# Gates and matrix-memory scores as three one-pass products, and the sample's key and query rows written before the gates

## The chip, the cores and the metric

The kernel runs on one core of one Trainium2 chip. The metric is the device time of one execution in microseconds (us). The time before is the median of three runs, 1539.87 us (1538.17 to 1540.1). Engines are called as the profile calls them: PE (matrix products), PEld (its weight loads), DVE (vector), ACT (scalar and activation functions), POOL, and SP, which here only issues DMAs.

## What is computed

One layer of a hybrid decoder, for a prompt of 256 tokens and a batch of 8 sample tokens: 264 columns together, in single precision. The parts that the change touches are the recurrent group (RG-LRU) and the mLSTM group, which share one projection `z = xn @ w_in`:

```python
xr, conv_new = causal_conv(z[..., OFF_RGX:OFF_RGG], conv_buf, conv_w, conv_b)
r = jax.nn.sigmoid(block_diag(xr, w_rg_a, b_rg_a))
ig = jax.nn.sigmoid(block_diag(xr, w_rg_x, b_rg_x))
h_rg, h_last = rglru(xr, r, ig, rg_lambda, h0)
y_rg = rmsnorm(h_rg * jax.nn.gelu(z[..., OFF_RGG:OFF_Q]), g_rg_out)
...
qk = jnp.einsum('bhtd,bhsd->bhts', qc, kc) * D
num = sc[..., None] * jnp.einsum('bhtd,bhdv->bhtv', qc, C) + jnp.einsum('bhts,bhsv->bhtv', qk, vc)
C_new = dec[..., None, None] * C + jnp.einsum('bhs,bhsd,bhsv->bhdv', w_end, kc, vc)
...
y_ml = rmsnorm(h_ml, g_ml_out) * jax.nn.sigmoid(z[..., OFF_O:OFF_I])
x = x + jnp.concatenate([y_rg, y_ml], axis=-1) @ w_out
```

`block_diag` is 8 blocks of 128 x 128 for each of the two gates. After this come cross attention to a memory of 256 tokens, a SwiGLU feed-forward part and a last norm.

## The kernel before

Everything is held transposed: 128 features on the partitions, the 264 tokens along the row. All large products run over weights that stream from HBM, in a list `steps` of 128-column blocks of 2048 rows. SP loads a step as two **pieces** of 1024 columns (tile `raw`, 5 buffers). ACT copies a piece to fp32r (the high part) and DVE subtracts to get the low part; both land in one tile `W`, of which there are **4 buffers**. PE then makes three one-pass fp32r products for each 128 x 128 block (`mm3`: high x high, high x low, low x high), 24 for a piece. A product of two plain fp32 tiles is also possible; the profile records it as two matmuls. I count pieces from 0: step s uses pieces 2s and 2s + 1, and because the ring has four tiles, piece n + 4 can be written only after PE has read all of piece n.

`w_in` is steps 0 to 40: 0 to 7 the RG-LRU input, 8 the mLSTM gates, 9 to 16 queries and keys, 17 to 24 values, 25 to 32 the gelu branch, 33 to 40 the mLSTM output gate. Results leave PSUM through DVE (`evac_...`).

Everything else runs as side threads (`side`, generators), which the step loop pumps: `pump` lets a thread go on while DVE's and ACT's estimated clocks are less than `SLACK` ahead of PE's. So the amount of side work decides in which step a thread's next part is issued. A scheduler then fixes one order of instructions for each engine, and each engine works through its order. Work with high priority (the splits above all) is moved forward. The threads that matter:

- `rg_gen` (L524): convolution `rg_conv`, the gates (16 fp32 products, two for each of 8 blocks), sigmoids, exponentials, square roots, scans.
- `ml_gates`, `ml_prompt` (the prompt's scores, two fp32 products for each head), `ml_values`, `ml_heads`.
- `ml_sample` (L815): the 8 sample tokens. It forms kd = key x input gate, transposes kd and the query to rows, writes them to HBM (`scr`) and reads them back spread over all partitions (`fetch`), and updates the matrix memory C for each head.
- `ml_norm` (L880), started at step 24 with the highest priority. It waits until `ml_heads` and `ml_sample` are done and step 33 is reached. Then it hands PE three kinds of small products by a queue of "drips", each due after so many further chunks of a step: `sums` (four, one for each head), `turn` (one, 19 chunks later: it transposes the normalising factor `f` to rows), and `scale` (four, 6 chunks later and then one each: they spread the rows `hl` that ACT and DVE make of `turn`'s result).

Two lines bind these drips to the steps. In `proj`, a step's first chunk is issued after the last drip:

```python
if c == 0:
    d = st.get("edge")
```

And `evac_o(j)` cannot go on without the scaled heads. It drains the queue if need be:

```python
finish(lambda: ml.get("nn", 0) > j // 2)
```

The loop holds the results of steps 33 to 35 back and evacuates them together after step 36's products (`if i == 36`). Whatever is left of the drips is then issued at once, in front of step 37.

Of the kernel before, what the change touches and what calls it, by code (L numbers as in the profile page):

```python
# [10 lines left out]
F32 = mybir.dt.float32  # L11
# [10 lines left out]
NS = 8  # L22
# [68 lines left out]
def layer_kernel(ctx: ExitStack, tc, xT, memT, vec, wrg, w_in, w_out, w_q, w_k, w_v, w_o,  # L91
# [398 lines left out]
    def evac_rgx(n):  # L490
        def f(ps):
            if "xr" not in rg:
                rg["xr"] = Arr(RGB)
            z = B([P, 2, 292])
            zi = z[:, 0, :]
            dve.memset(zi[:, 0:3], 0.0)
            smp = zi[:, 259:291].rearrange("p (b j) -> p b j", j=4)
            hist = V("cst", n * 24, 24).rearrange("p (b j) -> p b j", j=3)
            act.activation(smp[:, :, 0:3], hist, AF.Copy)
            dve.tensor_mul(zi[:, 3:259], ps[:, :T], rstd[:, :T])  # L500
            dve.tensor_mul(smp[:, :, 3:4], ps[:, T:N].rearrange("p (b j) -> p b j", j=1),
                           rstd[:, T:N].rearrange("p (b j) -> p b j", j=1))
            rg["z", n] = z
            if n >= 4:
                rg["zn"] = n + 1
        return f

    def rg_conv(n):
        z = rg.pop(("z", n))
        zi, t = z[:, 0, :], z[:, 1, :]  # L510
        smp = zi[:, 259:291].rearrange("p (b j) -> p b j", j=4)
        act.activation(cpo[:, n, :], zi[:, 256:259], AF.Copy)
        act.activation(cso[:, n, :, :], smp[:, :, 1:4], AF.Copy)
        w = [V("cw", j * 8 + n) for j in range(4)]
        dve.tensor_scalar(t[:, :288], zi[:, 0:288], w[0], V("cb", n), op0=OP.mult, op1=OP.add)
        dve.scalar_tensor_tensor(t[:, :288], zi[:, 1:289], w[1], t[:, :288], op0=OP.mult, op1=OP.add)
        dve.scalar_tensor_tensor(t[:, :288], zi[:, 2:290], w[2], t[:, :288], op0=OP.mult, op1=OP.add)
        xr = rg["xr"](n)
        dve.scalar_tensor_tensor(xr[:, :T], zi[:, 3:259], w[3], t[:, :T], op0=OP.mult, op1=OP.add)
        ts = t[:, 259:291].rearrange("p (b j) -> p b j", j=4)  # L520
        dve.scalar_tensor_tensor(xr[:, T:N].rearrange("p (b j) -> p b j", j=1), smp[:, :, 3:4], w[3],
                                 ts[:, :, 0:1], op0=OP.mult, op1=OP.add)

    def rg_gen():  # L524
        wr = [B([P, 8, P]), B([P, 8, P])]
        for j in range(2):
            sp.dma_start(wr[j], wrg[:, j * 8: j * 8 + 8, :])
        r, ig = Arr(RGB), Arr(RGB)
        for n in range(RGB):
            while rg["zn"] <= n:  # L530
                yield STEP
            rg_conv(n)
            yield STEP
            for t, j, b in ((r, 0, "ba"), (ig, 1, "bx")):
                ps = bank("ax")
                pe.matmul(ps[:, :N], wr[j][:, n, :], rg["xr"](n), start=True, stop=True)
                last = act.activation(t(n), ps[:, :N], AF.Sigmoid, bias=V(b, n))
            yield 0.1
        yield STEP
        xr, c = rg["xr"], rg["c"]  # L540
        e2 = Arr(RGB)

        for q in range(2):
            for n in range(4 * q, 4 * q + 4):
                with tc.issue_after(last.ins):
                    act.activation(e2(n), r(n), AF.Exp, scale=c[:, 8 + n: 9 + n])
                    le = act.activation(r(n), r(n), AF.Exp, scale=c[:, n: n + 1])
            dve.tensor_scalar(e2.tile(q), e2.tile(q), 1.0, -1.0, op0=OP.min, op1=OP.add)
            dve.tensor_mul(ig.tile(q), ig.tile(q), xr.tile(q))
            yield 2.0  # L550
        rg["le"] = le
        while "emc" not in ml:
            yield STEP
        for q in range(2):
            with tc.issue_after(ml["emc"].ins):
                act.activation(e2.tile(q), e2.tile(q), AF.Sqrt, scale=-1.0)
            dve.tensor_mul(ig.tile(q), ig.tile(q), e2.tile(q))
            yield 1.2
        h = Arr(RGB)
        rg["h"] = h  # L560
        for n in range(RGB):
            dve.tensor_tensor_scan(h(n)[:, :T], r(n)[:, :T], ig(n)[:, :T], 0.0, op0=OP.mult, op1=OP.add)
            yield 0.6
        h0 = V("h0", 0, 64).rearrange("p (n b) -> p n b", b=NS)
        for q in range(2):
            hq, rq_, iq = (t.tile(q)[:, :, T:N] for t in (h, r, ig))
            dve.tensor_mul(hq, rq_, h0[:, 4 * q: 4 * q + 4, :])
            dve.tensor_add(hq, hq, iq)
            act.activation(hlast[:, 4 * q: 4 * q + 4, :], h.tile(q)[:, :, T - 1: N], AF.Copy)
        pool_e.dma_start(o_h, hlast)  # L570
        pool_e.dma_start(o_cp, cpo)
        pool_e.dma_start(o_cs, cso)
        yield 0.3
# [106 lines left out]
    def evac_qk(j):  # L680
        def f(ps):
            if j == 0:
                ml["qk"] = Arr(8)
            if j < 4:
                dve.tensor_mul(ml["qk"](j), ps[:, :N], rstd)
            else:
                dve.scalar_tensor_tensor(ml["qk"](j), ps[:, :N], KSCALE, rstd, op0=OP.mult, op1=OP.mult)
            if j == 7:
                ml["sg"] = side(ml_sample(), 3)
                side(ml_prompt(), 2)  # L690
                side(ml_values(), 2)
                ml["pg"] = side(ml_heads(), 2)
        return f
# [8 lines left out]

    hT = {}

    def ml_prompt():
        qk = ml["qk"]
        yield STEP
        kt = B([P, 2, H, P])
        for tb in range(2):
            ps = bank("ax")  # L710
            for h in range(H):
                pe.transpose(ps[:, h * P: h * P + P], qk(4 + h)[:, tb * P: tb * P + P], ident)
            act.activation(kt[:, tb].rearrange("p h d -> p (h d)"), ps, AF.Copy)
            yield STEP
        while "gates" not in ml or not ml["gates"].done:
            yield STEP
        mhl = ml["mhl"]
        for h in range(H):
# [2 lines left out]
            pe.matmul(bc[:, :T], sel, mhl[:, 0], start=True, stop=False)  # L721
            pe.matmul(bc[:, :T], sel, mhl[:, 1], start=False, stop=True)
            sps = bank("ax")
            q, k = qk(h), qk(4 + h)
            pe.matmul(sps[:, 0:256], k[:, 0:P], q[:, 0:T], start=True, stop=True)
            pe.matmul(sps[:, 256:384], k[:, P:T], q[:, P:T], start=True, stop=True)
            w = B([P, 1024])
            E, Pm, kw = w[:, 0:384], w[:, 384:768], w[:, 768:1024]
            ml["w", h] = (Pm, kw, E[:, 0:P])
# [81 lines left out]

    snew = const.tile([P, H, NS], F32, name="snew")
    nums = const.tile([P, 8, NS], F32, name="nums")

    def ml_sample():  # L815
        while not ml["gates"].done:
# [1 line left out]
        qk = ml["qk"]  # L818
        ks, qs = qk.tile(1)[:, :, T:N], qk.tile(0)[:, :, T:N]
        sc, Dg = bcs[:, :, 0:8], bcs[:, :, 8:16]  # L820
        x = ltmp(64)
        kd, qc = (x[:, o: o + 32].rearrange("p (h b) -> p h b", b=NS) for o in (0, 32))
        dve.tensor_mul(kd, ks, Dg)
        dve.tensor_copy(qc, qs)
        n0 = V("n0", 0, 32).rearrange("p (h b) -> p h b", b=NS)
        dve.tensor_mul(snew, n0, sc)
        dve.tensor_add(snew, snew, kd)
        pool_e.dma_start(o_sn, snew)

        qn_ = ltmp(152)  # L830
        dve.memset(qn_[:, 0:120], 0.0)
        dve.tensor_mul(qn_[:, 120:152].rearrange("p (h b) -> p h b", b=NS), snew, qc)
        yield 0.6
        yield STEP
        ps = bank("ax")
        for h in range(H):
            pe.matmul(ps[:, h: h + 1], qn_[:, 8 * h: 8 * h + P], ones[:, 0:1], start=True, stop=True)
        pe.transpose(ps[0:64, 128:256], x, ident)
        yield STEP
        rows = ltmp(128)  # L840
        act.activation(rows[0:64, :], ps[0:64, 128:256], AF.Copy)
        act.activation(den.rearrange("p (h j) -> p h j", j=3)[:, :, 2:3],
                       ps[:, 0:4].rearrange("p (h j) -> p h j", j=1), AF.Abs)
        scr = drm.tile([64, P], F32, name="scr")
        pool_e.dma_start(scr, rows[0:64, :])
        yield 0.5
        def fetch(h, b4):
            C, kq = B([P, 4, 2, P]), B([P, 2, 4, P])
            pool_e.dma_start(C, c0T[h, :, b4 * 4: b4 * 4 + 4])
# [3 lines left out]
                pool_e.dma_start(kq[:, j].rearrange("p b d -> p (b d)"), src.partition_broadcast(P))  # L853
            return C, kq

        ahead = fetch(0, 0)
        yield STEP
        for h in range(H):
            while ml.get("vn", 0) < 2 * h + 2:
                yield STEP  # L860
            for b4 in range(2):
                C, kq = ahead
                n = 2 * h + b4 + 1
# [2 lines left out]
                for bb in range(4):  # L866
                    b = b4 * 4 + bb
                    t2 = tmp(256).rearrange("p (v d) -> p v d", d=P)
                    for vb in range(2):
                        act.activation(t2[:, vb, :], kq[:, 0, bb, :], AF.Copy,  # L870
                                       scale=ml["v"](2 * h + vb)[:, T + b: T + b + 1])
                    dve.scalar_tensor_tensor(C[:, bb], C[:, bb], sc[:, h, b: b + 1], t2, op0=OP.mult, op1=OP.add)
                    for vb in range(2):
                        dve.scalar_tensor_tensor(t2[:, 0, :], C[:, bb, vb, :], 1.0, kq[:, 1, bb, :], op0=OP.mult,
# [744 lines left out]
```

## Time and profile before

| | |
|---|---|
| time, median of 3 runs | 1539.87 us (1538.17 to 1540.1) |
| the profiled execution's own time | 1535.74 us |
| its span in the trace | 1534.0 us |
| busy: DVE, ACT, POOL | 69%, 51%, 8% of the span |
| DMA, mean | 215 GB/s |

The span is what the trace covers from the first to the last instruction; the profiled execution's own time is 1.74 us longer. An entry "A <- B: us, times, longest" in the waits says that A's engine sat idle until B finished. In the chain of waits and in the timeline a row is a start, a length, an engine, and a count of instructions. Ends of matmuls are modelled, so their costs are read from start to start. W, raw and ax are tile names: the split weights, the loaded weights, and the PSUM banks of the side work; mm are those of the steps.

### The profile page before, as it was taken

How to read it: one execution, taken by the hardware profiler on the slowest of the kernel's cores; microseconds unless marked ns; L12 is line 12 of the kernel's file. 1: busy time of each engine (PE TensorE's matmuls, PEld its weight loads, DVE VectorE, ACT ScalarE, POOL GpSimd, SP SyncE). 2: the span in 40 equal slices, each digit the busy share in tenths (PEclk: the TensorE clock that was granted, in tenths of full speed). 3: DMA queues.
4: the chain of work that ended last, by engine and by line, in shares of the span. 5: the costliest groups of instructions: out<-in, count | busy, mean ns of one | idle time of the engine just before them, and what ended most of it. 6: DMA issues, size and time to landing. Idle time of an engine off the chain costs nothing.

```text
span 1534.0 us, 29990 instructions
## 1 busy us (share of the span) xinstructions
PE 1524.8 (99%) x12028; PEld 1490.9 (97%) x12028; DVE 1059.3 (69%) x2013; ACT 784.0 (51%) x1234; POOL 126.1 (8%) x189
## 2 busy tenths in 40 slices
PE   9999999999999999999999999999999999999998
PEld 9999999999998888899999999999999999999997
DVE  7976988778898989966665555545555545555554
ACT  7555875655556666654444444334444433344463
POOL 0001210000223434400000000000000000000000
PEclk9999999999999999999999999999999999999999
DMA  8646996556798788755555555555555555555563
GB/s 300 203 154 203 322 327 207 194 179 233 266 341 326 246 339 332 248 160 188 188 180 182 190 179 184 188 179 184 188 179 185 187 180 186 185 180 186 158 225 121
DMA packets 94043, 329.17 MB, mean 215 GB/s; under 512 B 10992, under 2 KB 12448, under 8 KB 93904
## 3 DMA queue, kind: packets, MB, share of 16 engines
q1 hardware_dynamic: 78768, 274.62, 53.2%
q0 software_dynamic: 14992, 52.63, 9.7%
q8 instruction: 94, 1.54, 0.4%
q14 instruction: 45, 0.37, 0.1%
q10 hardware_dynamic: 144, 0.01, 0.0%
HBM read 314.36 MB, written 12.86 MB: 213 GB/s over the span
## 4 chain that ended last, share of the span: by engine, by line
PE 99%; DVE 0%; DMA 0%; ACT 0%; DVEq 0%; issue 0%; ACTq 0%
PE mm L63 94%; PE ax L63 5%; DVE B L63 0%; DMA raw<-w_in 0%; ACT W L63 0%; ACT B L63 0%; DVEq L1596 0%; ACTq L63 0%
## 5 line engine op out<-in xcount | busy, mean ns | idle before, releaser
L63 PE MATMUL mm<-B,W 128*128 128x264 f32 (+2 forms) x11008 | 1363.0, 285 | 0.0
L63 PEld LDWEIGHTS mm<-B,W 128*128 128x128 f32 x11008 | 1340.5, 188 | 11.7
L63 ACT ACTIVATE W<-raw 128x1024 fp32r<-128x1024 f32 (+2 forms) x520 | 536.7, 1034 | 640.3 <-PE mm L63 434.2
L63 DVE TENSOR_TENSOR W<-raw,W 128x1024 fp32r<-128x1024 f32 (+2 forms) x520 | 619.4, 1193 | 347.4 <-ACT W L63 346.0
L63 PE MATMUL mm<-W,B 128*128 128x512 f32 x384 | 92.4, 395 | 0.0
L63 PEld LDWEIGHTS mm<-W,B 128*128 128x128 f32 x384 | 70.9, 188 | 16.1
L63 DVE TENSOR_TENSOR t<-mm,rstd 128x264 f32<-128x264 f32 x104 | 44.7, 431 | 44.2 <-PE mm L63 44.1
L1511 POOL TENSOR_TENSOR B<-B,rstd 128x264 f32<-128x264 f32 x4 | 2.8, 738 | 854.1 <-ACT rstd L63 854.1
L63 DVE TENSOR_TENSOR xres<-xres,mm 128x264 f32<-128x264 f32 (+1 forms) x81 | 34.2, 423 | 37.8 <-PE mm L63 37.8
L63 DVE SCALAR_TENSOR_TENSOR B<-B,dw 128x256 f32<-128x256 f32 x128 | 53.8, 474 | 1.8 <-ACT dw L63 1.7
L63 DVE SCALAR_TENSOR_TENSOR dw<-B,qsm,dw 128x256 f32<-128x256 f32 x96 | 50.7, 537 | 2.3 <-ACT dw L63 1.9
L1142 POOL TENSOR_TENSOR dr<-dw,dr 128x256 fp32r<-128x256 f32 x32 | 38.4, 1200 | 102.7 <-ACT dr L63 102.6
L63 PE MATMUL ax<-B,B 128*128 128x256 f32 (+2 forms) x272 | 44.7, 303 | 0.0
L63 PEld LDWEIGHTS ax<-B,B 128*128 128x128 f32 x272 | 38.5, 190 | 2.4
L63 ACT ACTIVATE B<-xres,vecs 128x264 fp32r<-128x264 f32 (+1 forms) x64 | 31.0, 502 | 1.2 <-DMA xres<-xT 0.8
L1131 POOL DMA_DIRECT2D B<-kcT x32 | 17.4, 544 | 137.1 <-DVE B L63 127.2
L63 ACT ACTIVATE dw<-B,qsm 128x256 f32<-128x256 f32 x32 | 16.3, 508 | 22.4 <-DVE B L63 8.9
L63 ACT ACTIVATE B<-t 128x264 fp32r<-128x264 f32 (+1 forms) x60 | 24.5, 408 | 4.4 <-DVE t L63 4.4
L63 ACT ACTIVATE t<-xres 128x264 f32<-128x264 f32 (+2 forms) x46 | 18.7, 409 | 14.5 <-DVE xres L63 14.5
L63 ACT ACTIVATE t<-t 128x264 f32<-128x264 f32 (+1 forms) x61 | 24.7, 406 | 1.6 <-DVE t L63 1.5
L63 ACT ACTIVATE t<-B,B 128x128 f32<-128x128 f32 x64 | 20.1, 389 | 7.3 <-DMA B<-scr 7.3
L63 DVE SCALAR_TENSOR_TENSOR B<-xres,vecs,B 128x264 fp32r<-128x264 f32 x48 | 22.4, 486 | 0.6 <-ACT B L63 0.5
(166 smaller groups left out, 655.1 us busy)
## 6 DMA issues: line engine op xcount, KB each, us to landing
raw<-w_gu SPq DMA_DIRECT2D x176, 512.0 KB, 3.6
raw<-w_d SPq DMA_DIRECT2D x80, 512.0 KB, 3.6
raw<-w_in SPq DMA_DIRECT2D x78, 512.0 KB, 4.9
raw<-w_out SPq DMA_DIRECT2D x32, 512.0 KB, 3.7
raw<-w_q SPq DMA_DIRECT2D x32, 512.0 KB, 5.4
B<-kcT POOLq DMA_DIRECT2D x32, 512.0 KB, 8.3
B<-vcT POOLq DMA_DIRECT2D x32, 512.0 KB, 9.5
raw<-w_k SPq DMA_DIRECT2D x32, 512.0 KB, 6.5
```

The source lines that it names most:

```text
L63: return f(*a, **k)
L1131: pool_e.dma_start(kc, kcT[h, b])
L1142: pool_e.tensor_sub(wr[:, 1], acc, wr[:, 0].bitcast(F32))
L1511: e.tensor_mul(st["y"](c), st["y"](c), r)
```

## The change

Four edits:

1. The gates' weights are split once into high and low parts (4 tiles `gw`); each convolved block is split as well (`xh`, `xl`), and each gate becomes an `mm3` of three products.
2. The prompt's queries and keys are split (4 tiles `qk2`), and each score product becomes an `mm3`, 256 and 128 columns wide.
3. The sample's keys and queries are copied, transposed and written to `scr` in `ml_prompt`, without the gate; the gate Dg multiplies the values instead (`vds`). `fetch(0, 0)` waits for that write alone, and `ml_prompt` has priority 1 in place of 2.
4. Buffers: three blocks of the convolution's input share a tile, and so do three of its results.

```diff
     def rg_gen():
         wr = [B([P, 8, P]), B([P, 8, P])]
         for j in range(2):
             sp.dma_start(wr[j], wrg[:, j * 8: j * 8 + 8, :])
+        yield STEP
+        gw = {}
+        for q in range(2):
+            for j in range(2):
+                gw[j, q] = B([P, 4, 2 * P], F32R, skip=48)
+                src = wr[j][:, 4 * q: 4 * q + 4, :]
+                act.activation(gw[j, q][:, :, 0:P], src, AF.Copy)
+                dve.tensor_sub(gw[j, q][:, :, P:], src, gw[j, q][:, :, 0:P].bitcast(F32))
+                yield 0.7
...
             rg_conv(n)
+            if n % 2 == 0:
+                x2 = B([P, 4, N], F32R)
+            xh, xl = x2[:, n % 2 * 2, :], x2[:, n % 2 * 2 + 1, :]
+            act.activation(xh, rg["xr"](n), AF.Copy)
+            dve.tensor_sub(xl, rg["xr"](n), xh.bitcast(F32))
             yield STEP
             for t, j, b in ((r, 0, "ba"), (ig, 1, "bx")):
                 ps = bank("ax")
-                pe.matmul(ps[:, :N], wr[j][:, n, :], rg["xr"](n), start=True, stop=True)
+                w = gw[j, n // 4][:, n % 4, :]
+                mm3(ps[:, :N], (w[:, 0:P], w[:, P:]), (xh, xl), True, True)
...
-                side(ml_prompt(), 2)
+                side(ml_prompt(), 1)
...
     def ml_prompt():
         qk = ml["qk"]
-        yield STEP
+        xr = ltmp(64)
+        for j in range(2):
+            dve.tensor_copy(xr[:, 32 * (1 - j): 32 * (1 - j) + 32].rearrange("p (h b) -> p h b", b=NS),
+                            qk.tile(j)[:, :, T:N])
+        yield STEP
+        ps = bank("ax")
+        pe.transpose(ps[0:64, 0:P], xr, ident)
+        rows = ltmp(128)
+        act.activation(rows[0:64, :], ps[0:64, 0:P], AF.Copy)
+        pool_e.dma_start(scr, rows[0:64, :])
+        ml["scr"] = True
...
+        qk2 = []
+        for h in range(H):
+            x = B([P, 4, T], F32R, skip=32 * (h % 2))
+            qk2.append(x)
+            for j, y in enumerate((qk(h), qk(4 + h))):
+                act.activation(x[:, 2 * j], y[:, :T], AF.Copy)
+                dve.tensor_sub(x[:, 2 * j + 1], y[:, :T], x[:, 2 * j].bitcast(F32))
+            yield 0.8
...
-            pe.matmul(sps[:, 0:256], k[:, 0:P], q[:, 0:T], start=True, stop=True)
-            pe.matmul(sps[:, 256:384], k[:, P:T], q[:, P:T], start=True, stop=True)
+            qh, ql, kh, kl = (qk2[h][:, j] for j in range(4))
+            mm3(sps[:, 0:256], (kh[:, 0:P], kl[:, 0:P]), (qh, ql), True, True)
+            mm3(sps[:, 256:384], (kh[:, P:T], kl[:, P:T]), (qh[:, P:T], ql[:, P:T]), True, True)
...
     def ml_sample():
...
-        dve.tensor_mul(kd, ks, Dg)
-        dve.tensor_copy(qc, qs)
...
+        while "scr" not in ml:
+            yield STEP
         ahead = fetch(0, 0)
+        kd = ltmp(32).rearrange("p (h b) -> p h b", b=NS)
+        dve.tensor_mul(kd, ks, Dg)
...
+            vd = vds[:, h % 2]
+            dve.tensor_mul(vd, ml["v"].tile(h // 2)[:, h % 2 * 2: h % 2 * 2 + 2, T:N],
+                           Dg[:, h: h + 1, :].to_broadcast([P, 2, NS]))
...
                     for vb in range(2):
                         act.activation(t2[:, vb, :], kq[:, 0, bb, :], AF.Copy,
-                                       scale=ml["v"](2 * h + vb)[:, T + b: T + b + 1])
+                                       scale=vd[:, vb, b: b + 1])
```

The change also moves the side threads against the steps. The first place is PE's order at a gate pair, RG-LRU block 5 (a row is one instruction, out<-in and its size; x3 is three in a row). Before:

```order
L63 MATMUL mm_1192<-B_183,W_1097 128x264
L63 MATMUL ax_1245<-B_1010,B_586 128x264
L63 MATMUL ax_1248<-B_1010,B_587 128x264
L63 MATMUL mm_1266<-B_144,W_1186 128x264
L63 MATMUL mm_1266<-B_145,W_1186 128x264
```

The same place, at the end of piece 27, with the change (here block 4):

```order
L63 MATMUL mm_1200<-B_185,W_1137 128x264
L63 MATMUL ax_1253<-B_1110,B_712 128x264 x3
L63 MATMUL ax_1259<-B_1110,B_715 128x264 x3
L63 MATMUL mm_1299<-B_146,W_1194 128x264
L63 MATMUL mm_1299<-B_147,W_1194 128x264
```

Each single row of the gates has become three, and the gates come one block later against the pieces.

The second place is PE's order around `ml_norm`'s `turn` (the rows that read a `c` tile) and `scale` (the rows that read `ident_r`). Before, `turn` stands in the middle of piece 73, whose tile is W_3115:

```order
L63 MATMUL ax_3110<-ident,c_3109 4x128 x2
L63 MATMUL ax_3110<-ident,c_3109 4x8
L63 MATMUL mm_3208<-B_183,W_3115 128x264
L63 MATMUL mm_3208<-B_184,W_3115 128x264
L63 MATMUL mm_3208<-B_183,W_3115 128x264 x2
L63 MATMUL mm_3208<-B_184,W_3115 128x264
L63 MATMUL mm_3208<-B_183,W_3115 128x264 x2
L63 MATMUL mm_3208<-B_184,W_3115 128x264
L63 MATMUL mm_3208<-B_183,W_3115 128x264 x2
L63 MATMUL mm_3208<-B_184,W_3115 128x264
L63 MATMUL mm_3208<-B_183,W_3115 128x264
L63 MATMUL ax_3265<-B_3111,ident_r 128x264
```

With the change, where piece 73 is W_3215 and piece 74 is W_3277:

```order
L63 MATMUL mm_3283<-B_185,W_3215 128x264
L63 MATMUL ax_3275<-ident,c_3274 4x128 x2
L63 MATMUL ax_3275<-ident,c_3274 4x8
L63 MATMUL ax_3371<-B_3276,ident_r 128x264
L63 MATMUL ax_3376<-B_3276,ident_r 128x264
L63 MATMUL ax_3381<-B_3276,ident_r 128x264
L63 MATMUL ax_3386<-B_3276,ident_r 128x264
L63 MATMUL ax_3381<-B_3276,ident_r 128x264
L63 MATMUL ax_3376<-B_3276,ident_r 128x264
L63 MATMUL ax_3371<-B_3276,ident_r 128x264
L63 MATMUL ax_3386<-B_3276,ident_r 128x264
L63 MATMUL mm_3424<-B_146,W_3277 128x264
```

`turn` has moved from the middle of piece 73 to its end, and the 12 products of the piece that stood between it and `scale` now stand ahead of both.

The third place is DVE's order there: the last Newton steps of the factor `f` (the `c` tiles) and the splits of the weights (W<-raw). Before, W_3312 is piece 76:

```order
L63 SCALAR_TENSOR_TENSOR c_3109<-c_3163,c_3109 128x12
L63 TENSOR_TENSOR c_3163<-c_3109 128x12
L63 SCALAR_TENSOR_TENSOR c_3163<-c_3163,c_3108 128x12
L63 SCALAR_TENSOR_TENSOR c_3109<-c_3163,c_3109 128x12
L63 TENSOR_TENSOR c_3109<-c_3109,c_3107 128x12
L63 TENSOR_TENSOR W_3312<-raw_3198,W_3312 128x8x128
L63 TENSOR_TENSOR B_3111<-ax_3110,B_3111 4x264
```

With the change, W_3421 is piece 77, mm_3283 is the result of pieces 72 and 73, and B_1841 is the RG-LRU state that is scaled by its norm:

```order
L63 TENSOR_TENSOR t_3412<-mm_3283,rstd 128x264
L63 SCALAR_TENSOR_TENSOR c_3328<-c_3328,c_3273 128x12
L63 SCALAR_TENSOR_TENSOR c_3274<-c_3328,c_3274 128x12
L63 TENSOR_TENSOR c_3328<-c_3274 128x12
L63 SCALAR_TENSOR_TENSOR c_3328<-c_3328,c_3273 128x12
L63 TENSOR_TENSOR W_3421<-raw_3269,W_3421 128x8x128
L63 TENSOR_TENSOR B_1841<-B_1841,lt_3101 128x264 x2
L63 SCALAR_TENSOR_TENSOR c_3274<-c_3328,c_3274 128x12
L63 TENSOR_TENSOR B_1841<-B_1841,lt_3101 128x264
L63 TENSOR_TENSOR c_3274<-c_3274,c_3272 128x12
L63 TENSOR_TENSOR B_3276<-ax_3275,B_3276 4x264
```

The factor's last write, c_3274<-c_3274,c_3272, used to stand ahead of the split of piece 76. It now stands behind the split of piece 77 and behind the evacuation of piece 73's own result.

More of the change, by code (lines that the diff above doesn't have):

```diff
@@ L493, in f @@
                 rg["xr"] = Arr(RGB)
-            z = B([P, 2, 292])
-            zi = z[:, 0, :]
+            if ("zt", n // 3) not in rg:
+                rg["zt", n // 3] = B([P, 3, 292])
+            z = zi = rg["zt", n // 3][:, n % 3, :]
             dve.memset(zi[:, 0:3], 0.0)
@@ L508, in rg_conv @@
     def rg_conv(n):
-        z = rg.pop(("z", n))
-        zi, t = z[:, 0, :], z[:, 1, :]
+        zi = rg.pop(("z", n))
+        if n % 3 == 0:
+            rg["t"] = B([P, 3, 292])
+        t = rg["t"][:, n % 3, :]
         smp = zi[:, 259:291].rearrange("p (b j) -> p b j", j=4)
@@ L703, in layer_kernel @@
     hT = {}
+    scr = drm.tile([64, P], F32, name="scr")
     def ml_prompt():
         qk = ml["qk"]
+        xr = ltmp(64)
+        for j in range(2):
+            dve.tensor_copy(xr[:, 32 * (1 - j): 32 * (1 - j) + 32].rearrange("p (h b) -> p h b", b=NS),
+                            qk.tile(j)[:, :, T:N])
         yield STEP
+        ps = bank("ax")
[4 more added lines that the diff above has]
+        ml["scr"] = True
         kt = B([P, 2, H, P])
@@ L723, in ml_prompt @@
             sps = bank("ax")
-            q, k = qk(h), qk(4 + h)
-            pe.matmul(sps[:, 0:256], k[:, 0:P], q[:, 0:T], start=True, stop=True)
-            pe.matmul(sps[:, 256:384], k[:, P:T], q[:, P:T], start=True, stop=True)
+            qh, ql, kh, kl = (qk2[h][:, j] for j in range(4))
+            mm3(sps[:, 0:256], (kh[:, 0:P], kl[:, 0:P]), (qh, ql), True, True)
+            mm3(sps[:, 256:384], (kh[:, P:T], kl[:, P:T]), (qh[:, P:T], ql[:, P:T]), True, True)
             w = B([P, 1024])
@@ L813, in layer_kernel @@
     nums = const.tile([P, 8, NS], F32, name="nums")
+    vds = const.tile([P, 2, 2, NS], F32, name="vds")
     def ml_sample():
@@ L820, in ml_sample @@
         sc, Dg = bcs[:, :, 0:8], bcs[:, :, 8:16]
-        x = ltmp(64)
-        kd, qc = (x[:, o: o + 32].rearrange("p (h b) -> p h b", b=NS) for o in (0, 32))
-        dve.tensor_mul(kd, ks, Dg)
-        dve.tensor_copy(qc, qs)
[L825 to L833, printed above, removed]
-        yield STEP
[L835 to L846, printed above, removed]
         def fetch(h, b4):
@@ L854, in fetch @@
             return C, kq
+        while "scr" not in ml:
+            yield STEP
         ahead = fetch(0, 0)
+        kd = ltmp(32).rearrange("p (h b) -> p h b", b=NS)
+        dve.tensor_mul(kd, ks, Dg)
+        n0 = V("n0", 0, 32).rearrange("p (h b) -> p h b", b=NS)
+        dve.tensor_mul(snew, n0, sc)
+        dve.tensor_add(snew, snew, kd)
+        pool_e.dma_start(o_sn, snew)
+        qn_ = ltmp(152)
+        dve.memset(qn_[:, 0:120], 0.0)
+        dve.tensor_mul(qn_[:, 120:152].rearrange("p (h b) -> p h b", b=NS), snew, qs)
+        yield 0.6
+        yield STEP
+        ps = bank("ax")
+        for h in range(H):
+            pe.matmul(ps[:, h: h + 1], qn_[:, 8 * h: 8 * h + P], ones[:, 0:1], start=True, stop=True)
+        yield STEP
+        act.activation(den.rearrange("p (h j) -> p h j", j=3)[:, :, 2:3],
+                       ps[:, 0:4].rearrange("p (h j) -> p h j", j=1), AF.Abs)
         yield STEP
```

## The prediction

> **What bounds the kernel now.** I read the page first, then the waits, then the chain, and last the timeline where the order of work changes.
>
> ```profile
> PE 1524.8 (99%) x12028; PEld 1490.9 (97%) x12028; DVE 1059.3 (69%) x2013; ACT 784.0 (51%) x1234; POOL 126.1 (8%) x189
> ...
> PE 99%; DVE 0%; DMA 0%; ACT 0%; DVEq 0%; issue 0%; ACTq 0%
> ...
> PE mm L63 <- DVE ones L63: 1.1, 1, 1.1
> PE ax L63 <- ACT B L63: 0.4, 1, 0.4
> ```
>
> PE is busy for 99% of the span and is 99% of the chain. All its waits together are 1.5 us, at the start. So time can change in two ways only: PE gets more or less work, or PE begins to wait. Whether it begins to wait depends on how far the others run ahead, here between 36 and 260 us, where all edits lie:
>
> ```profile
> ACT W L63 <- PE mm L63: 43.1, 31, 3.8
> ...
> DVE W L63 <- ACT W L63: 19.0, 19, 2.5
> ...
> ACT t L63 <- DMA B<-scr: 7.3, 2, 5.0
> ```
>
> ACT waits 31 times for PE to free a weight tile: the splits run as far ahead as the ring of four lets them. That lead covers side work, as long as PE asks for nothing that stands behind a split it is itself holding back.
>
> **PE's work.** Rows of the chain: start, length, count.
>
> ```profile
> 100.04 5.77 PE mm L63 x48
> 106.71 17.24 PE mm L63 x144
> ...
> 146.62 5.76 PE mm L63 x48
> 153.66 5.75 PE mm L63 x48
> ```
>
> A one-pass product of 264 columns takes 5.77 / 48 = 0.120 us. Between 105.81 and 106.71 stand two fp32 gates: 0.90 us. Six one-pass products are 0.72. Eight pairs: 8 x (0.72 - 0.90) = **-1.4 us**.
>
> Scores, from the timeline:
>
> ```profile
> 152.31 0.50 PE L63 MATMUL ax<-B,ident_r 4*128 4x256 f32 x2
> 152.74 0.92 PE L63 MATMUL ax<-B,B 128*128 128x256 f32 x4
> 153.41 5.99 PE L63 MATMUL mm<-B,W 128*128 128x264 f32 x48
> ```
>
> From the first score record to the next product: 0.67 us for one product 256 wide and one 128 wide. By width the fp32 gate's 0.45 gives 0.44 and 0.22. The three 256-wide one-pass products are at most 3 x 0.12 = 0.36. A one-pass product with only 128 columns is not in the trace. Bounds: half an fp32 one, 0.11 (its one record), up to all of it, 0.22. So a head costs 0.36 + 0.33 to 0.66, against 0.67: four heads lose 0.1 to 1.4 us. I take 0.1, by the single record as the nearest row, and keep 1.4 for the range. PE's work: -1.4 + 0.1 = **-1.3 us**.
>
> **What lies beside PE.** The new splits, with rows of the same sizes:
>
> ```profile
> L63 DVE TENSOR_TENSOR W<-raw,W 128x512 fp32r<-128x512 f32 x24 | 16.2, 686 | 1.5 <-ACT W L63 1.4
> L63 DVE TENSOR_TENSOR B<-t,B 128x264 fp32r<-128x264 f32 x44 | 18.7, 426 | 0.0
> ...
> L63 ACT ACT_TABLE_LOAD x12 | 15.4, 1283 | 1.4 <-PEq L1591 1.2
> ```
>
> DVE gets 4 x 0.69 + 16 x 0.43 = 9.6 us, ACT about as much, and two more table loads, 2.6 us. They fall between 40 and 150 us and use up the splits' lead there. The key and query rows go out one step earlier: two copies, a transpose, an ACT copy, the DMA to `scr`, then the fetch of C and two reads of `scr`; on POOL's queue these now precede `o_sn` and `o_h`, for which nobody waits. ACT's wait for `scr` (longest 5.0 us) moves ahead by about one step, to a place ahead of piece 45's split. I price all this at nothing: 43.1 us of waiting for PE stand against some 12 us of work. If the cover fails at one place, around the first scores, 1 to 2 us are lost. Below nothing it can't go, since PE waits for none of it today.
>
> **The new wait.** Only one place has PE ask for something behind a split that it holds back itself. Today, from the chain:
>
> ```profile
> 246.16 0.57 PE ax L63 x6
> 246.72 1.66 PE mm L63 x12
> 248.38 1.15 PE ax L63 x8
> 249.54 12.53 PE mm L63 x103
> ```
>
> `turn` (0.57), 12 products, `scale` (1.15). The 12 products cover the round trip from `turn` to `scale`:
>
> ```profile
> 246.76 0.38 ACT L63 ACTIVATE B<-ax 4x264 fp32r<-4x264 f32 x1 [0.89 <-PE ax L63]
> 247.17 0.42 DVE L63 TENSOR_TENSOR B<-ax,B 4x264 fp32r<-4x264 f32 x1
> ...
> 248.47 1.06 ACT L63 ACTIVATE W<-raw 128x1024 fp32r<-128x1024 f32 x1 [1.33 <-PE mm L63]
> ```
>
> The rows for `scale` are there at 247.59, 0.87 us after `turn` ends at 246.72. And at 248.47, as soon as piece 73 is read, ACT splits piece 77.
>
> With the change the sums come one step later. Step 36's evacuation then drains the queue, and `turn` and `scale` stand together behind piece 73's last product. Ahead of `turn`'s input DVE now has, in its fixed order, the evacuation of piece 73's result, four small steps, the split of piece 77, three scalings of the RG-LRU state and two small steps. Neither of the first and third can start before PE ends piece 73. Call that moment T0. The timeline has all kinds of these on DVE, start to start:
>
> ```profile
> 241.88 0.43 DVE L63 TENSOR_TENSOR t<-mm,rstd 128x264 f32<-128x264 f32 x1 [0.33 <-PE mm L63]
> 242.23 0.16 DVE L63 TENSOR_TENSOR c<-c 128x12 f32<-128x12 f32 x1
> 242.43 0.38 DVE L63 SCALAR_TENSOR_TENSOR c<-c,c 128x12 f32<-128x12 f32 x2
> 242.84 0.17 DVE L63 TENSOR_TENSOR c<-c 128x12 f32<-128x12 f32 x1
> 243.03 1.22 DVE L63 TENSOR_TENSOR W<-raw,W 128x1024 fp32r<-128x1024 f32 x1
> 244.17 0.37 DVE L63 SCALAR_TENSOR_TENSOR c<-c,c 128x12 f32<-128x12 f32 x2
> ```
>
> 0.35 + 0.80 + 1.14 (243.03 to 244.17) + 3 x 0.35 (the first row's kind of size) + 2 x 0.20 = 3.7 us. With some 0.3 us for semaphores and for DVE being late with piece 76, PE starts `turn` at **T0 + 4.0**. Behind `turn` the round trip is now bare: + 0.9, and 0.1 for the last semaphore. PE loses 4.0 + 1.0 = **5.0 us**. Bounds: 4.2, if DVE is free at T0 and all overlaps, to 5.8, if DVE is late by another 0.8.
>
> **The clock.** The windows at the end show what PE's silence does (columns: busy of PE, PEld, DVE, ACT, POOL, then PEclk, the granted clock):
>
> ```profile
> 1526.00:1527.00 1.00, 0.38 (x2) 0.00 (x0) 1.00 (x4) 0.39 (x1) 1.00 (x2) 1.00 0.78 269
> 1527.00:1528.00 1.00, 0.00 (x0) 0.00 (x0) 1.00 (x4) 0.00 (x0) 1.00 (x2) 1.00 0.93 352
> 1528.00:1529.00 1.00, 0.00 (x0) 0.00 (x0) 0.94 (x3) 0.00 (x0) 0.75 (x2) 0.86 1.03 393
> 1529.00:1530.00 1.00, 0.00 (x0) 0.00 (x0) 0.00 (x0) 0.00 (x0) 0.00 (x0) 0.50 1.02 385
> ```
>
> The last matmul ends at 1526.38; 0.86 is the mean of full and half clock, so it fell at 1528.72, after 2.3 us. A gap of 4.0 us can do this. The price, from the chain's start:
>
> ```profile
> 5.34 4.85 PE ax L63 x20
> ...
> 19.40 2.91 PE ax L63 x24
> ```
>
> 20 products take 4.85 us there, against 20 x 0.121 = 2.4: **+2.2 us** I take for one such ramp (less than 2.4, since the first of them also wait for splits). [...]
>
> **Sum.** The profiled execution: 1534.0 - 1.3 + 5.0 + 2.2 = 1539.9 us of span, or 1535.74 + 5.9 = 1541.6 of its own time. The three runs' median lies 4.13 us above that execution; I add the same 5.9 to the median: **1545.8 us**.
>
> **Rivals.**
> - *The wait without the clock's fall.* Against it: 2.3 us were enough at the end. [...] 1539.87 + 3.7 = 1543.6.
> - *Not slower.* The wait at T0 is shorter, because DVE's rows overlap, or ACT splits piece 77 out of a tile freed before T0. Without the split and the wait for it the row sum is 2.5 us, the loss 3.5, and the net 1539.87 - 1.3 + 3.5 = 1542.1, with no clock fall. It decides at a loss of 4.4 us: below, the net is under 3.1 us, which is 0.2% and about what a measurement of this kernel can tell from no change. Against it: at 248.47 the split waits for PE.
> - *No wait at all; the change does what it says.* PE's work alone, 1538.6. It would need `turn`'s factor ready at T0, which the order excludes.
> - *More waits.* ACT's wait for `scr` delays piece 45 and the first scores by 1 to 2 us, and the 128-wide products cost 1.3 more: up to 1549.
>
> **How the numbers follow.** The wait with the fall 0.50, without it 0.28, not slower 0.10, no wait 0.05, more waits 0.07. The range takes the first two, the upper bounds, and most of the third: 1541.5 to 1549. Slower by over 0.2% (above 1542.95): 0.50 + 0.07 + 0.20 of the 0.28 = 0.77. Within 0.2%: 0.20. Faster: 0.03, if side work freed elsewhere shortens something that the trace doesn't show.
>
> **What would show it.** Right: PE's waits gain one of 3.5 to 4.5 us on DVE's c tile and one of about 1 us on DVE's B, both near 245 us, and PEclk under 1.00 just behind them; gate triples at 0.36 us. Wrong: PE without waits there; scores at over 1 us a head; waits of PE on W or B between 115 and 155 us.

## The result and the profile after

The changed kernel takes **1542.01 us** (median of 14 runs, 1541.03 to 1542.79). The kernel before, run beside it, has a median of 1536.9 us (14 runs, 1535.36 to 1540.1). The ratio is **1.0031**, with a 95% interval of 1.0023 to 1.0038: slower by about 4.8 us (0.0031 x 1536.9). The two profiled executions differ by 1541.54 - 1535.74 = 5.8 us, their spans by 1539.6 - 1534.0 = 5.6 us.

First the waits of the changed kernel, PE's alone (who waited, for whom, us in total, times, longest):

```profile
PE ax L63 <- DVE c L63: 3.7, 1, 3.7
PE mm L63 <- DVE ones L63: 1.1, 1, 1.1
PE ax L63 <- ACT B L63: 1.1, 2, 0.6
PE mm L63 <- ACT W L63: 0.2, 1, 0.2
```

The first row is new: one wait of 3.7 us for a `c` tile, the factor that `turn` transposes. The third has grown by one wait of about half a microsecond. The chain of waits shows where they stand (start, length, what):

```profile
243.63 3.00 PE mm L63 x24
246.63 0.03 ACTq L63
246.66 0.04 issue
246.70 1.06 ACT W L63
247.76 0.02 issue
247.79 1.23 DVE W L63
249.01 0.69 DVE B L63 x2
...
250.04 0.18 DVE c L63
250.22 0.14 issue
250.35 1.06 PE ax L63 x6
251.42 0.02 issue
251.44 0.39 ACT B L63
251.83 0.04 issue
251.87 2.13 PE ax L63 x8
```

Read it downwards. PE ends the 24 products of piece 73 at 246.63. That frees a weight tile, and ACT writes the high half of piece 77 into it (1.06), DVE the low half (1.23). Behind it, in DVE's fixed order, stand three scalings of the RG-LRU state and two small steps, and the last of these writes the one value that PE asks for. So PE was waiting behind a split that it had itself held back. At 250.35 `turn` starts, and from its end to `scale` PE has nothing but ACT's copy to wait for. Before the change, 12 products stood there.

Then the windows (columns: busy of PE, PEld, DVE, ACT, POOL, then PEclk):

```profile
249.00:250.00 1.00, 0.00 (x0) 0.00 (x0) 1.00 (x5) 0.00 (x0) 0.00 (x0) 1.00 0.22 90
250.00:251.00 1.00, 0.65 (x4) 0.42 (x5) 0.21 (x2) 0.00 (x0) 0.00 (x0) 0.65 0.92 283
251.00:252.00 1.00, 0.53 (x5) 0.34 (x3) 0.15 (x1) 0.38 (x1) 0.00 (x0) 0.50 0.58 217
...
257.00:258.00 1.00, 1.00 (x9) 1.00 (x9) 1.00 (x4) 1.00 (x4) 0.00 (x0) 0.94 0.00 0
```

The windows left out all have 0.50. A window's PEclk is a mean of 1.00 and 0.50, so 0.65 puts the fall at 250.30 (0.70 of that window is slow) and 0.94 the return at 257.12 (0.12 of it is slow): 6.8 us at half clock. All times of falls below are read in this way. `turn` takes 1.06 us there instead of 0.57, `scale` 2.13 instead of 1.15.

Last the terms that should save. From the chain, a gate pair, and from the timeline, a head's scores and the product behind them:

```profile
72.40 0.72 PE ax L63 x6
```

```profile
150.38 0.90 PE L63 MATMUL ax<-B 128*128 128x256 f32 x6
151.12 1.65 PE L63 MATMUL mm<-B,W 128*128 128x264 f32 x12
```

A pair takes 0.72 us (0.89 before), a head's scores 151.12 - 150.38 = 0.74 (0.67 before). The first product behind the scores is quicker, though: from its record to the next are 0.174 us, and before 0.205, so a head costs 0.03 to 0.07 more.

### The profile page after: what moved, and what is told of

Same layout as the page of the kernel before. It is cut to its first block, busy times and chain, and to the rows that moved or that the text cites. A ratio compares the mean times of both kernels' runs of the same rounds, so it can differ in the third digit from the quotient of the medians.

```text
span 1539.6 us, 30086 instructions
## 1 busy us (share of the span) xinstructions
PE 1525.6 (99%) x12052; PEld 1492.0 (97%) x12052; DVE 1068.5 (69%) x2038; ACT 794.0 (52%) x1256; POOL 126.8 (8%) x189
## 4 chain that ended last, share of the span: by engine, by line
PE 97%; DMA 1%; DVE 1%; issue 0%; ACT 0%; DVEq 0%; ACTq 0%
PE mm L63 93%; PE ax L63 4%; DMA xres<-xT 1%; DVE B L63 0%; DMA raw<-w_in 0%; DVE W L63 0%; ACT B L63 0%; DMA vecs<-vec 0%; ACT W L63 0%; DVE acc_x L63 0%; DVEq L1632 0%; DVE c L63 0%; ACTq L63 0%; DVEq L63 0%
## 5 line engine op out<-in xcount | busy, mean ns | idle before, releaser
L63 PE MATMUL ax<-B,B 128*128 128x256 f32 (+2 forms) x272 | 40.2, 288 | 0.0
L63 DVE TENSOR_TENSOR B<-B,B 128x264 fp32r<-128x264 f32 (+8 forms) x36 | 22.7, 650 | 5.9 <-ACT B L63 5.9
L63 ACT ACTIVATE t<-B,vds 128x128 f32<-128x128 f32 x64 | 20.5, 389 | 8.3 <-DVE B L63 4.7
```

Of the source, the lines that this page charges most:

```text
L63: return f(*a, **k)
```

## Experiments

Each kernel was timed beside the kernel before on the same chip. Ratios are to that kernel, with 95% intervals; its median was 1536.06 to 1536.15 us in the three sessions.

**1. The sums in piece 70 again, by force.** The changed kernel plus:

```diff
         st["i"] = i
+        if i == 33:
+            finish(lambda: ml["pg"].done and ml["sg"].done)
```

> The changed kernel, with one addition: at step 33 the side threads ml_prompt and ml_sample are run to their end, so that ml_norm's sums stand in piece 70 again and turn in the middle of piece 73, as before the change. Theory (the loss is the wait in front of turn, with the fall of the clock behind it): the 3.7 us wait on DVE's c tile and PEclk 0.50 near 250 us are gone, and with them 7.0 us; what is left is PE's work, -1.1 to -1.3 us against the kernel before (ratio 0.9993). Rival (the added work of DVE and ACT costs its time wherever it stands): still 4 to 5 us above the kernel before (ratio 1.003), with the waits at another place.

Measured: 1538.73 us, ratio 1.0014 (1.0005 to 1.0022). The wait in front of `turn` is gone, but PE has new ones:

```profile
PE mm L63 <- DVE B L63: 1.9, 1, 1.9
...
PE ax L63 <- DVE B L63: 0.5, 1, 0.5
```

Of the 4.8 us, 2.6 are won back (0.0017 x 1536); neither theory's number came out, though a wait at another place did appear, as the rival had it. In this kernel's order the RG-LRU norm's two products, which stood behind piece 69, come behind `scale`, and its scalings come so late that step 41, the first to read them, waits at 272.7 for 1.9 us. And the clock fell there too:

```profile
273.00:274.00 1.00, 0.00 (x0) 0.00 (x0) 1.00 (x3) 1.00 (x3) 0.00 (x0) 1.00 0.00 0
...
275.00:276.00 1.00, 1.00 (x9) 1.00 (x8) 1.00 (x4) 1.00 (x4) 0.00 (x0) 0.81 0.94 311
...
278.00:279.00 1.00, 1.00 (x6) 1.00 (x6) 1.00 (x3) 0.00 (x0) 0.00 (x0) 0.50 0.04 12
279.00:280.00 1.00, 1.00 (x10) 1.00 (x9) 0.90 (x4) 0.52 (x1) 0.00 (x0) 0.98 0.99 369
```

It fell at 275.62, when PE had been at work again for 1.1 us, and came back at 279.04: a gap of 1.9 us was followed by 3.4 us at half clock. This is not so in every execution: of the eleven, seven (the profiled one among them) have a mean granted clock of 0.997 or 0.998 and spans of 1536.2 to 1537.8 us, the other four 0.999 and 1535.3 to 1536.0. So the place of `turn` accounts for its wait; the edit that moved it displaced something else.

**2. The wait filled with work.** The changed kernel with 30 unused products in front of `turn`:

```diff
         def turn():
+            d = st["last"]
+            for k in range(30):
+                with tc.issue_after(d.ins):
+                    d = pe.matmul(ps[:, 16: 16 + N], ones_r, rx(0)[0], start=True, stop=True)
```

> The changed kernel with 30 products of 264 columns (3.6 us of work whose result nobody reads) between piece 73's last product and turn: PE is busy through most of the wait, and nothing else is moved. Theory (wait and clock are two prices, 4.1 and 2.9 us): PE's wait for DVE's c tile shrinks to 0.6 us or less, PEclk stays at 1.00, and the time is 2.9 us under the changed kernel's: about 2 us above the kernel before (ratio 1.0013). Rival (PE's slow products behind the wait have another cause, such as late operands): they stay slow, and the time stays about 5 us above the kernel before.

Measured: 1538.71 us, ratio 1.0015 (1.0005 to 1.0024). The chain, and a window:

```profile
246.53 3.66 PE ax L63 x30
250.18 0.09 issue
250.27 0.65 PE ax L63 x6
...
251.38 1.33 PE ax L63 x8
```

```profile
251.00:252.00 1.00, 0.62 (x4) 0.58 (x5) 0.42 (x1) 0.32 (x1) 0.00 (x0) 1.00 0.29 115
```

`turn` still starts at 250.27: the wait is as long as before, only filled. The clock stays at 1.00 in this profile, and the span is 1539.6 - 1536.8 = 2.8 us shorter. That is the price of the clock; by the times it is 3.3 us (1542.01 - 1538.71, two sessions) or by the ratios 0.0016 x 1536 = 2.5. Two of the eleven executions have a mean clock of 0.997 and took 1540.5 us; there the clock may have fallen all the same.

**3 and 4. Which edit makes the sums late.** Experiment 3 is the kernel before with edits 1 and 4 alone, experiment 4 the changed kernel without edit 1. The core of each:

```diff
-                pe.matmul(ps[:, :N], wr[j][:, n, :], rg["xr"](n), start=True, stop=True)
+                w = gw[j, n // 4][:, n % 4, :]
+                mm3(ps[:, :N], (w[:, 0:P], w[:, P:]), (xh, xl), True, True)
```

```diff
-                w = gw[j, n // 4][:, n % 4, :]
-                mm3(ps[:, :N], (w[:, 0:P], w[:, P:]), (xh, xl), True, True)
+                pe.matmul(ps[:, :N], wr[j][:, n, :], rg["xr"](n), start=True, stop=True)
```

> The kernel before with edits 1 and 4 alone (gates as three one-pass products, shared buffers); scores, scr and the priority stay. Theory (the gates' splits delay ml_sample by a step): sums stand in piece 72, and the wait of 3 to 4 us in front of turn and the fall of the clock are here too; -1.4 us of PE's work + 7 = about 5 us above the kernel before (ratio 1.003). Rival (the move of scr and the priority make the sums late): no wait, 1.4 us under the kernel before (ratio 0.9991).

> The changed kernel with the gates as two-record fp32 products again (edit 1 undone; scores, scr, priority and buffers as changed). Theory: sums in piece 70, no wait in front of turn, PEclk 1.00; scores cost PE 0.74 us a head against 0.67: +0.3 us against the kernel before (ratio 1.0002). Rival (the move of scr and the priority make the sums late): 6 to 7 us above the kernel before (ratio 1.004).

Measured: gates alone 1543.06 us, ratio 1.0045 (1.0032 to 1.0057), with the same wait of 3.7 us; without the gates 1535.79 us, ratio 0.9997 (0.9988 to 1.0005), with no wait of PE behind the first 8 us. So edit 1, the one that saves PE work, makes the sums late. It adds work for DVE and ACT (splits of 4 x 0.69 + 8 x 0.43 = 6.2 us on DVE, about as much on ACT) and takes work from PE; either lets the side threads fall behind by the pump's rule, and no run separates the two. One size stays open: gates alone are 1 us slower than the whole change. In their profile the clock was down for 10.2 us (249.64 to 259.88) and not for 6.8, but experiment 11 shows that the whole change has such executions too. Without the gates the span is 1533.1, 0.9 under that of before, where +0.3 was expected; the times have 0.3 less, inside their interval. Most of this lies ahead of the scores: piece 14 starts at 46.94 in that execution and at 47.59 before (-0.65), piece 75 at 251.96 and 252.45 (-0.49), so between the two it lost 0.16, about the 0.1 to 0.3 that the scores cost.

**5. Late sums without the change.** The kernel before, with:

```diff
-        while not (ml["pg"].done and ml["sg"].done) or st["i"] < 33:
+        while not (ml["pg"].done and ml["sg"].done) or st["i"] < 34:
```

> The kernel before, without any of the four edits, with one number changed: ml_norm waits for step 34 in place of 33, so that its sums stand in piece 72 and turn and scale behind piece 73, as in the changed kernel. Theory (the place of turn is the whole loss): wait of about 3.7 us on DVE's c tile, PEclk 0.50 behind it, 6.9 to 8 us above the kernel before (ratio 1.0045 to 1.005). Rival (the split work of gates and scores is needed for the wait): within 1 us of the kernel before.

Measured: 1543.6 us, ratio **1.0047** (1.0033 to 1.0061), 7.4 us above the kernel before. PE's waits and the clock:

```profile
PE ax L63 <- DVE c L63: 3.7, 1, 3.7
PE ax L63 <- ACT B L63: 1.2, 2, 0.8
```

```profile
250.00:251.00 1.00, 0.00 (x0) 0.00 (x0) 1.00 (x5) 0.00 (x0) 0.00 (x0) 0.62 0.26 78
...
260.00:261.00 1.00, 1.00 (x9) 1.00 (x8) 1.00 (x4) 0.85 (x2) 0.00 (x0) 0.76 0.00 0
```

One number, none of the edits, and the whole loss is there: the place of `turn` is enough for it.

**6 and 9. The change with its sums in time, and the control.** One number in the changed kernel (6), the same in the kernel before (9):

```diff
-    SLACK = 0.5
+    SLACK = 0.6
```

> The changed kernel with one number changed: SLACK 0.6 in place of 0.5, which lets the side threads run 0.1 us further ahead; the sums stand in piece 70 and turn in the middle of piece 73 again, and the RG-LRU norm keeps its place in front of the sums (with the threads run to their end at step 33 it was displaced). Theory: no wait over 0.6 us on PE behind the start, PEclk 1.00 to the end; PE's work alone is left, 1.1 to 1.3 us under the kernel before (ratio 0.9992). Rival (the change's side work makes a new wait wherever the old one is taken away): 1.5 us or more above the kernel before (ratio over 1.001).

> The kernel before with SLACK 0.6 and nothing else: the control for the changed kernel with SLACK 0.6 (ratio 0.9989). Theory (that gain is PE's shorter gates, and SLACK only puts turn back): no change, ratio 0.9995 to 1.0005. Rival (the gain is SLACK's own): about 1 us faster, ratio 0.999.

Measured: the changed kernel **1535.05 us**, ratio 0.9989 (0.998 to 0.9998); the kernel before 1536.37 us, ratio 0.9999 (0.999 to 1.0008). PE's waits in the first:

```profile
PE mm L63 <- DVE ones L63: 1.1, 1, 1.1
PE ax L63 <- ACT B L63: 0.5, 1, 0.5
```

With `turn` back in the middle of piece 73 the change is 1.1 us faster than the kernel before (1536.15 - 1535.05), and neither kernel has a wait of PE behind the start: this is PE's work. In the trace piece 76 starts 1.13 us earlier than before (254.19 against 255.32), though 0.27 of it were there at piece 14. Between the changed kernel with 0.5 and with 0.6 lie 1542.01 - 1535.05 = 7.0 us by the medians and (1.0031 - 0.9989) x 1536 = 6.5 by the ratios.

**7. Gates alone with SLACK 0.6** (the two edits shown):

> Gates alone (edits 1 and 4) with SLACK 0.6: sums in piece 70. Theory: as the kernel above without the 0.3 us that the scores cost: 1.4 us under the kernel before (ratio 0.9991). Rival (gates alone cost more by themselves, as their 7 us with the wait against 5 us for the whole change might be read): 0.5 us or more above the kernel before.

Measured: 1536.15 us, ratio 0.9998 (0.999 to 1.0007): neither. Its profile and that of experiment 9 have a wait that experiment 6 lacks. The chain of experiment 9 (the steps between the first and the last three are left out):

```profile
147.14 7.88 DMA B<-scr
...
161.31 0.36 DVE B L63
161.66 0.04 issue
161.71 0.66 PE ax L63 x4
```

In experiment 9 a read of `scr` of 7.9 us comes ahead of DVE's work for a head's transposes, and PE waits 1.1 us for them. Experiment 7 has a wait of 1.0 us at the same place, but there the chain runs over ACT's work and not over the read. For experiment 7 the sum fits: gates -1.4 and the wait +1.0 leave -0.4, and -0.3 was measured. For experiment 9 it doesn't: its median is only 0.3 us above the kernel before (1536.37 against 1536.06), and the profiled execution is the slowest of its eleven (1537.58), so the wait need not be in all of them. Why gates alone gain nothing is not settled. In experiment 6, where the rows are written earlier, PE has no such wait; that edit 3 takes it away is possible but not shown, since the scores differ too.

**8. Half of the wait filled.** Experiment 2 with `range(15)`.

> The changed kernel with 15 unused products (1.8 us) between piece 73 and turn in place of 30: PE then stands still for about 2.1 us. [...] If a gap of 2 us is enough (it was 1.9 us at 272 us in the kernel with the threads run to their end), PEclk shows 0.50 for 3.4 us or more, and the time is 1.5 to 3 us longer than with 30 products (ratio 1.0025 to 1.0035).

Measured: 1541.4 us, ratio 1.0029 (1.0018 to 1.004); PE's wait is 1.9 us. The clock:

```profile
253.00:254.00 1.00, 1.00 (x7) 0.86 (x7) 1.00 (x4) 0.00 (x0) 0.00 (x0) 0.84 0.00 0
...
257.00:258.00 1.00, 1.00 (x10) 1.00 (x9) 1.00 (x4) 1.00 (x4) 0.00 (x0) 0.96 0.00 0
```

It fell at 253.68, 2.9 us after `turn` had started (at 250.81), and rose at 257.08. Half of the wait filled won 0.6 us (1542.01 - 1541.4), all of it 3.3. The gap is not the only thing ahead of this fall: between it and 253.22 stand `turn`, a wait of 0.5 us and `scale`. Which of them brought it, no run shows.

**10. A cheaper form of the scores.** Experiment 6 with the 128 x 128 score as one fp32 product again:

```diff
-            mm3(sps[:, 256:384], (kh[:, P:T], kl[:, P:T]), (qh[:, P:T], ql[:, P:T]), True, True)
+            pe.matmul(sps[:, 256:384], qk(4 + h)[:, P:T], qk(h)[:, P:T], start=True, stop=True)
```

> The changed kernel with SLACK 0.6 and the 128 x 128 scores as plain fp32 products again; the 256-wide ones stay one-pass. From the trace of the changed kernel the three one-pass products of 128 columns take 0.28 us and the fp32 one 0.22: 4 x 0.06 = 0.24 us less PE work than with SLACK 0.6 alone (ratio to the kernel before 0.9988 against 0.9989, which the times can't tell apart; the trace can: 0.58 us a head for the scores in place of 0.74, if the 0.22 holds, -0.36 us at most). Rival (a one-pass product of 128 columns costs no more when it stands among others): 0.74 us a head as before or more.

Measured: **1534.53 us**, ratio 0.9983 (0.9974 to 0.9992), the fastest of all; against experiment 6 the intervals overlap, so the times don't tell the two apart; the trace does. From the timeline:

```profile
152.38 0.62 PE L63 MATMUL ax<-B 128*128 128x256 f32 x3
152.84 0.38 PE L63 MATMUL ax<-B,B 128*128 128x128 f32 x2
152.98 0.37 PE L63 MATMUL mm<-B,W 128*128 128x264 f32 x1
```

From the first score to the next product: 0.60 us, against 0.74 and, before the change, 0.67; with the slower first product behind fp32 (0.205) 0.80 against 0.91 and 0.88. So in this place the one-pass form pays at 256 columns and not at 128.

**11. The changed kernel once more.**

> [...] Rival (the length of the slow stretch follows the wait): 6.8 us again, since the wait is the same. Time 4.5 to 7 us above the kernel before (ratio 1.003 to 1.0045).

Measured: 1541.96 us, ratio 1.0035 (1.0021 to 1.0049), the wait 3.7 us again. The clock:

```profile
249.00:250.00 1.00, 0.00 (x0) 0.00 (x0) 1.00 (x3) 0.00 (x0) 0.00 (x0) 0.61 0.34 139
...
259.00:260.00 1.00, 1.00 (x9) 1.00 (x8) 1.00 (x3) 1.00 (x4) 0.00 (x0) 0.77 0.00 0
```

It fell at 249.22 and rose at 259.46: 10.2 us at half clock, with the same wait of 3.7 us that the first profile has with 6.8. So the wait alone does not set the length. This execution took 1542.76 us, the first one 1541.54.

**12. The factor ahead of the evacuation on DVE.**

```diff
             z = tmp()
-            dve.tensor_mul(z, ps[:, :N], rstd)
+            if j == 3:
+                with tc.issue_after(st["fac"].ins):
+                    dve.tensor_mul(z, ps[:, :N], rstd)
+            else:
+                dve.tensor_mul(z, ps[:, :N], rstd)
```

> The changed kernel with DVE's evacuation of piece 73's result issued behind the factor of turn; the scheduler then puts the four small steps ahead of the split of piece 77 too, and only that split, two scalings and one small step stand between PE's end of piece 73 and turn. By the prediction's sum of DVE's own rows the wait becomes 1.14 + 0.70 + 0.20 + 0.3 = 2.4 us. By the changed kernel's chain, in which DVE's split starts only when ACT's half of piece 77 is done, 1.1 us after PE's end of piece 73, it becomes 1.1 + 1.14 + 0.70 + 0.2 + 0.1 = 3.2 us, since evacuation and small steps lay beside ACT's half. PEclk falls to 0.50 in both cases, as it did with a gap of 1.9 us.

Measured: the wait is 3.3 us (one execution, 1543.18 us). The chain:

```profile
244.60 3.00 PE mm L63 x24
...
247.67 1.06 ACT W L63
248.73 0.02 issue
248.76 0.04 DVE W L63
```

DVE had its small steps done and stood waiting for ACT. Without DVE's evacuation ahead of the split, the path from PE's end of piece 73 runs over ACT's half of it: 3.3 is the chain's number (3.2), not that of DVE's rows (2.4). The 0.4 us that were won are a scaling and a small step that no longer stand ahead. The time did not fall with the wait: the clock was down for 10.2 us here (250.06 to 260.30).

## Why the prediction was right

The mechanism, the place and the sign were as forecast, and the time lay in the range. By its steps:

- **PE's work, -1.3 us.** Piece 73's first product starts at 244.56 before and at 243.49 with the change, with the same work ahead of it: -1.07, in an execution that was 0.2 late already at piece 14 (47.79 against 47.59): -1.27. Gates: 8 x (0.72 - 0.89) = -1.4, as worked out. Scores: 4 x 0.03 to 4 x 0.07 = +0.1 to +0.3, at the 0.1 taken and far from the 1.4 kept for the range. Of the three one-pass products of 128 columns (150.84 to 151.12, 0.28 us together) two take the 0.11 of the nearest row, the first 0.06.
- **What lies beside PE, nothing.** Right in both profiles of the changed kernel: no wait of PE between 40 and 240 us. Two table loads came, as read from the order.
- **The new wait, 5.0 us.** Right in kind. PE began `turn` at 250.35, 3.7 us after the end of piece 73 (4.0 forecast). The sum of rows came out near, partly by luck. It had DVE's evacuation and four small steps (0.35 + 0.80) ahead of the split and gave ACT's half of the split (1.06) no place. In the trace the two lie beside each other. ACT's half ends at 247.76 (246.70 + 1.06). DVE's rows:

```profile
246.65 0.43 DVE L63 TENSOR_TENSOR t<-mm,rstd 128x264 f32<-128x264 f32 x1 [0.32 <-PE mm L63]
...
247.61 0.17 DVE L63 SCALAR_TENSOR_TENSOR c<-c,c 128x12 f32<-128x12 f32 x1
247.79 1.23 DVE L63 TENSOR_TENSOR W<-raw,W 128x1024 fp32r<-128x1024 f32 x1
```

The last small step ends at 247.78: a tie. Experiment 12 takes the DVE rows away, and ACT's half holds the split back just as long, which the sum of rows would not have given. The bare round trip was 0.5 us rather than 1.0, since `scale`'s first product starts as soon as ACT's row is there (251.83) and does not wait for DVE's. The forecast's 0.3 us for semaphores and for DVE's lateness and its 0.1 for the last semaphore were the author's estimates, from no row; the `issue` steps of the chain that the section on the result shows are 0.02 to 0.14 us each. Together PE lost 4.2 us to waits where 5.0 were forecast.
- **The clock, +2.2 us.** Right that it falls; the size was low. Filled with work, the wait cost 2.8 us of span less (experiment 2). The 2.2 us were read from 20 products of 0.24 us near the start of the execution; the windows there (0 to 12 us) have a PEclk of 1.00, so that the clock made them slow was the author's estimate and no window shows it. Measured with this wait are 6.8 to 10.2 us at a PEclk of 0.50. The rival without the fall (1543.6) lost: the clock fell in all four profiles that have the wait at its full length, 3.7 us after PE's last product in the first and 2.0 to 2.7 us after it in experiments 3, 5 and 11. The chance of 0.28 that this rival was given was the author's estimate.
- **The sum.** Wait and clock were forecast at 7.2 us. From piece 73 to piece 76 (261.23, before 255.32: +5.91, from -1.07) the trace loses 7.0; by the times, experiment 6 has 6.5 to 7.0 and experiment 5 has 7.4. The two terms' errors, 0.8 too much and 0.6 too little, nearly cancel: that the total fits to 0.2 is luck.
- **The absolute time** was 1545.8 in the forecast and 1542.01 in the runs, 0.5 us above the low end of the range. It lies next to the number of the rival that was not slower (1542.1), and under the 1542.95 from which the forecast called it slower, though the trace has the forecast's mechanism. The step that failed is the last: the 5.9 us were added to a median of three runs, 1539.87, and 14 runs of the same kernel have 1536.9. From there the forecast would have been 1542.8. The profiled execution (1541.6 forecast, 1541.54 measured) was the better anchor. As a difference, 5.9 was forecast; measured are 4.8 by the ratio, 5.1 by the medians and 5.8 between the profiled executions.

The change did what it says on PE, and 7 us were lost where it touches no line. Its gain of about 1.3 us would be 0.1%; with `turn` back in place 1.1 us are there by the medians.

## What to carry to other kernels

When side work sets in which step a dependent part is issued, a few microseconds of it can push that part past a fixed point of the program. Look at what the program drains there, and whether PE then asks for a value that stands, on its producer's engine, behind a step that waits for PE. Where such a margin hangs on one number (here a slack of 0.5 or 0.6), try the number before judging the change.

## What the runs showed of the hardware

- **The granted clock and PE's waits.** In all seven profiles with a wait of PE of 1.9 us or more near 250 or 272 us, PEclk went from 1.00 to 0.50 during the wait or after it, and stayed there longer than the wait had lasted: 3.4 us with the waits of 1.9 us (experiments 1 and 8), 6.8 us in the first profile and 10.2 us in experiments 3, 5 and 11 with waits of 3.7 us, 10.2 us with the 3.3 us of experiment 12. So the wait alone does not set the length.
- **When it fell.** The fall came 2.0 us after PE's last product in experiment 11, 2.5 to 2.7 in experiments 12, 3 and 5, 3.7 in the first profile. In experiment 1 it was 2.9 us, and PE had been at work again for the last 1.1 of them; in experiment 8 `turn`, a wait of 0.5 us and `scale` lay between the wait of 1.9 us and the fall. In experiment 2, whose waits of PE there are 0.5 us at most, the windows from 240 to 300 us have a PEclk of 1.00. What sets the moment of the fall and how long it lasts, no run shows.
- **One-pass products of 128 columns took nearly as long as those of 256.** In the first scores of the changed kernel those of 256 columns follow each other in 0.12 us; of the three with 128 columns the last two still take 0.11 each. What limits them, no run shows.
